# Latent attention in a two-block network: rotary tables built during the feed forward, another order of the projections, one square for four heads, and an exponential issued early

## The chip, the cores and the metric

The kernel runs on one core of one Trainium2 chip. The metric is the device time of one execution in microseconds (us). Differences below about 0.2% (2.5 us of this kernel) can't be told from no change.

## The reference

The network runs 256 tokens of width 1024 through two blocks of two layers each. The first block has a mixer of dilated attention and a state-space scan, then one of gated linear recurrences, each followed by a SwiGLU feed forward of hidden width 2816. The second block has a layer of latent attention and one of grouped-query attention, each with attention over 256 memory tokens beside it, and a feed forward behind each. The change touches mainly the latent attention:

```python
def _mla_mixer(p, q_a_norm, w_q_b, kv_a_norm, w_kv_b, q_norm, k_norm, rope):
    c_q, c_kv, k_pe = p[..., :384], p[..., 384:640], p[..., 640:704]
    q = (_rmsnorm(c_q, q_a_norm) @ w_q_b).reshape(B, S, 8, 128 + 64)
    kv = (_rmsnorm(c_kv, kv_a_norm) @ w_kv_b).reshape(B, S, 8, 128 + 128)
    q_nope = _rmsnorm(q[..., :128], q_norm[:128])
    q_pe = _apply_axial_rope(_rmsnorm(q[..., 128:], q_norm[128:]), rope)
    k_nope = _rmsnorm(kv[..., :128], k_norm[:128])
    v = kv[..., 128:]
    k_pe = _apply_axial_rope(_rmsnorm(k_pe, k_norm[128:])[:, :, None, :], rope)[:, :, 0, :]
    return _blocked_attention([q_nope, q_pe], [k_nope, k_pe], v, 192 ** -0.5)
```

Each head's 128 columns of queries and keys are normalised by their own mean square, and 64 more columns are rotated by tables of cosines and sines (times the norm's gain). The memory queries and the grouped queries are normalised by head too, which needs sums of squares of four heads of 128 columns at a time.

## The kernel before, in words

Tokens lie on the 128 partitions in two halves (`HALVES`). Every product is computed in three matmuls of reduced-precision pieces (`mm3`, L299): the operand and the weights are each split into a high and a low part. A weight tile of 128x1024 holds two blocks of 512 columns; it comes by a DMA of the SP queue into `wr`, ScalarE (ACT) copies it into the high part `wh`, and VectorE (DVE) subtracts to get the low part `wl` (`weights`, L283). Six such pairs and four raw tiles are in flight.

`linear` (L393) issues the weights, then the matmuls of the first half of the tokens, then of the second; behind each half a `sink` takes the PSUM bank (`pm`; there are six) through ACT, DVE and GpSimd (POOL). The sinks of the latent layer, all inside `mla_layer` (L1454):

- `nope_sink` (L1500), for four heads of 128 queries or keys: `normed_heads` (L685) sums the squares of each head (`head_sumsq`, L668), POOL raises them to the power -1/2 (`rsqrt`, L412), DVE multiplies the bank by the factors into a slot `s`, and then TensorE (PE) transposes it into `pt` (against `ident`) and ACT copies it out.
- `rope_sink` (L1513), for the rotated part of all eight heads: the same with eight heads of 64, then `axial` (L770), seven DVE instructions with the tables `rt`, then the transposes.
- `q_mem_sink` (L737) copies the bank, and forms factors of four heads.

`head_sumsq` has two ways: for more than four heads one ACT square over all columns into a scratch tile `j` (there is one such tile) and a DVE reduction (L677); for four or fewer one ACT square for each head, with an accumulated output that a second small ACT instruction reads.

The order of the work is written out by hand. `pe_time` counts the matmuls' modelled time; `later(delay, fn, writes)` queues a step, `poll` (after each `mm3`) issues those that are due, and `need(keys)` forces the steps that write a key. The delays are in `TUNE`: `noden` and `nodego` for the scaling and the transposes of `nope_sink`, `ropen` and `ropego` for the rotary part. The first attention job of the latent layer (`start`, L613) needs the rotated key and queries and the first four heads of plain queries and keys. It is spread right behind the linear that makes the second four heads of keys. The framework's planner then orders each engine's instructions by its own costs, so that one that is written later may stand earlier in its engine's queue.

The order of the linears in the latent layer is: latent queries (3 blocks of 128), latent keys and values with the rotated key, memory queries (L1493), first keys (L1538), rotated queries (L1539), first queries, first values, second keys; then the jobs begin. `rope_tables` (L1438), called at the head of each attention layer, loads gains, cosines and sines, and forms eight products on DVE. The feed forward is `ffn` (L504): its up half runs in chunks of 256 columns with a Silu each, its down half in `rows_out`; an `aside` is called behind its first 512 columns.

Of the kernel before, what the change touches and what calls it, by code (L numbers as in the profile page):

```python
# [9 lines left out]
F32 = mybir.dt.float32  # L10
F32R = mybir.dt.float32r
I32 = mybir.dt.int32
AF = mybir.ActivationFunctionType
# [4 lines left out]
P = 128  # L18
D = 1024
KD = D // P  # L20
FF = 2816
EPS = 1e-6
HALVES = (0, 1)
# [35 lines left out]
    "mqgo": 1.0,  # L59
    "mkn": 3.0,  # L60
    "noden": 2.3,
    "nodego": 3.5,
    "ropen": 2.5,
    "ropego": 5.0,
    "kpego": 3.5,
    "gkn": 2.0,
    "gkgo": 4.0,
# [7 lines left out]
    "conv": 2.3,  # L75
    "mem": 8.0,
    "rows": 2.0,
    "s5a": 0.0,
    "s5ad": 2.0,
    "s5b": 4.5,  # L80
# [61 lines left out]
class Net:  # L142
# [358 lines left out]
            tiles.append(t)  # L501
        return tiles

    def ffn(self, X, r, gate, up, g_at, u_at, down, post, gains, last=False, aside=None):  # L504
        nc = self.nc
        HT = Operand(self, FF // P)
        wg = self.weights([(gate, k * P, g_at, g_at + 512) for k in range(KD)])
        wu = self.weights([(up, k * P, u_at, u_at + 512) for k in range(KD)])
        for h in HALVES:
            G, U = self.group(X, h, wg, 512), self.group(X, h, wu, 512)  # L510
            s, t = self.slot(), self.slot()
            self.act(s, G, AF.Silu, scale=r[h])
            self.mul(t, U, s)
            self.to_features(HT, h, 0, [t[:, i * P : (i + 1) * P] for i in range(4)])
        rows, key = self.spread_rows(r)
        if aside is not None:
            aside()
        mean = [self.sm() for h in HALVES]
        for h in HALVES:
            self.ts(mean[h], r[h], math.sqrt(1.0 / D), ALU.mult)  # L520
        two = lambda a: a.rearrange("p (a q) -> p a q", a=2)
        both = rows.unsqueeze(1).to_broadcast([P, 2, 256])
        for c0 in range(512, FF, 256):
            G = self.wide_t(X, gate, g_at + c0)
            self.need(key)
            s, t = self.slot(), self.slot()
            self.wide_sum(s, G)
            self.mul(two(s), two(s), both)
            self.act(s, s, AF.Silu)
            U = self.wide_t(X, up, u_at + c0)  # L530
            self.wide_sum(t, U)
            self.mul(t, t, s)
            self.heads_out(HT, c0 // P, t)
        gp = None if post is None else self.load_post(post)
        KF = FF // P
        self.flush()
        return self.rows_out(HT, down, range(KF), 5, gp, gains, last, r, mean)
# [130 lines left out]
    def head_sumsq(self, src, nh, dh, r=None):  # L668
        w = self.sm(nh)
        scale = math.sqrt(1.0 / dh)  # L670
        if r is not None:
            scale = self.sm()
            self.ts(scale, r, math.sqrt(1.0 / dh), ALU.mult)
        sq = self.junkt()
        if nh > 4:
            self.act(sq[:, : nh * dh], src, AF.Square, scale=scale)
            self.nc.vector.tensor_reduce(  # L677
                out=w, in_=sq[:, : nh * dh].rearrange("p (n d) -> p n d", n=nh), axis=AX.X, op=ALU.add
            )
        for i in range(nh if nh <= 4 else 0):  # L680
            self.act(sq[:, i * dh : (i + 1) * dh], src[:, i * dh : (i + 1) * dh], AF.Square, scale=scale, accum_out=w[:, i : i + 1])
        self.ts(w, w, EPS, ALU.add)
        return w
# [754 lines left out]
    def rope_tables(self, src, dim, nq):  # L1438
# [4 lines left out]
            self.nc.sync.dma_start(out=pk[i], in_=self.ins[src][i])  # L1443
        at = lambda j: pk[j * dim // 512][:, (j * dim) % 512 : (j * dim) % 512 + dim]
        tabs = {}
        for i, who in enumerate(("q", "k")):
            for h in HALVES:
                C, S = (self.rtab.tile([P, dim], F32, name=self.name("rt"), tag=f"rt{who}{h}{j}") for j in range(2))
                self.mul(C, at(2 * h), at(4 + 2 * i))
                self.mul(S, at(2 * h + 1), at(5 + 2 * i))  # L1450
                tabs[who, h] = (C, S)
        return tabs

    def mla_layer(self, X, R):  # L1454
        tabs = self.rope_tables("rope64", 64, 8)
        CQ, CKV = Operand(self, 3), Operand(self, 2)
        rq, rkv = [None, None], [None, None]

# [31 lines left out]
        self.linear(X, "mla_w_in", 0, 384, latent(CQ, rq, 3, "q_a"))  # L1490
        self.linear(X, "mla_w_in", 384, 704, kv_sink)
        mem = {}
        self.linear(X, "mla_w_in", 704, 1216, self.q_mem_sink(0, R, mem))  # L1493

        qT, kT, V = self.big(), self.big(), self.big()
        qpT = [self.slot(), self.slot()]
# [38 lines left out]
        heads = [job(n) for n in range(8)]  # L1535
        jobs = self.attention(heads[:4] + self.memory_jobs(0, mem, self.mem_kv[0], 8) + heads[4:], Y)
        self.share = TUNE["mla_share"]
        self.linear(CKV, "w_kv_b", 0, 512, nope_sink(kT, rkv, "k_nope", 0, "k"))  # L1538
        self.linear(CQ, "w_q_b", 1024, 1536, rope_sink)  # L1539
        self.linear(CQ, "w_q_b", 0, 512, nope_sink(qT, rq, "q_nope", 0, "q"))  # L1540
        self.linear(CKV, "w_kv_b", 1024, 1536, v_sink(0))
        self.linear(CKV, "w_kv_b", 512, 1024, nope_sink(kT, rkv, "k_nope", 4, "k"))
# [9 lines left out]


    def gqa_layer(self, X, R):
        tabs = self.rope_tables("rope128", 128, 8)
        Y = Operand(self, 12)
        qT, kT, V = self.big(), self.slot(), self.slot()
        head = lambda T, n: T.rearrange("p (n t) -> p n t", n=n)
# [29 lines left out]
        mem = {}  # L1588
# [21 lines left out]
    def run(self):  # L1610
# [19 lines left out]
        self.dump("x_b", X, R)  # L1630
        X, R = self.odd_mixer(X, R)
        self.dump("x_c", X, R)
        X, R = self.ffn(X, R, "gate1", "up1", 0, 0, "down1", 3, "mix2_0")
        self.dump("x_d", X, R)

        X, R = self.mla_layer(X, R)
        self.dump("x_e", X, R)
        X, R = self.ffn(X, R, "gu2_0", "gu2_0", 0, FF, "down2_0", None, "mix2_1")
        self.dump("x_f", X, R)
        X, R = self.gqa_layer(X, R)  # L1640
        self.dump("x_g", X, R)
# [196 lines left out]
```

## Time and profile before

| what | value |
|---|---|
| time, median of 3 runs | 1258.91 us (1258.33 to 1259.23) |
| the profiled execution's own time | 1257.49 us |
| its span from the first to the last instruction | 1255.7 us |
| PE busy, share of the span | 1238.2 us, 99% |
| DVE busy | 879.7 us, 70% |
| ACT busy | 766.5 us, 61% |
| granted clock of PE, mean | 0.999 |
| matmuls | 6526 |

The durations of matmuls overlap, so a busy PE says only that one was under way; what PE loses is read from the distance of one matmul's start to the next one's. An idle time in brackets names the engine and line that ended it. L217 is the helper of every activation, L195 of every two-operand DVE instruction, L208 and L209 of DVE's tensor_scalar, L220 of every matmul, L227 of every transpose, L414 is `rsqrt`: the tile names tell which is which.

### The profile page before, as it was taken

What the parts mean: (1) busy time and instruction counts of PE and PEld (TensorE: products, weight loads), DVE (VectorE), ACT (ScalarE), POOL (GpSimd) and SP (SyncE); (2) the same over time, 40 slices, a digit from 0 to 9 for tenths busy, and PEclk for the clock granted to TensorE, in tenths of its full rate; (3) what the DMA queues carried; (4) which work ended last, traced back from release to release, by engine and by line L of the source; (5) the groups of instructions that cost most, each with busy time, mean ns of one, the idle gap of its engine ahead of it and who ended that gap; (6) DMA issues with size and microseconds to landing.
All of it is one profiled execution on the core that took longest, in us unless ns stands there. A gap on an engine that the chain in (4) does not pass through costs nothing.

```text
span 1255.7 us, 17972 instructions
## 1 busy us (share of the span) xinstructions
PE 1238.2 (99%) x6526; PEld 1036.8 (83%) x6526; DVE 879.7 (70%) x1579; ACT 766.5 (61%) x1446; POOL 52.3 (4%) x64
## 2 busy tenths in 40 slices
PE   8999999999999999999999999999999999999998
PEld 6776888888889788888887788888888888888887
DVE  7897578775588977776477855777746865677752
ACT  6767577554488766555378845555536675655541
POOL 1000000000000100000013100000000100000000
PEclk9999999999999999999999999999999999999999
DMA  8614357666555556666545224656664532666562
GB/s 272 228 54 149 119 200 235 192 193 207 160 184 173 166 187 219 190 193 203 183 151 177 85 68 151 211 191 188 210 191 152 182 118 81 201 199 191 186 196 71
DMA packets 63065, 216.83 MB, mean 173 GB/s; under 512 B 7136, under 2 KB 7520, under 8 KB 62976
## 3 DMA queue, kind: packets, MB, share of 16 engines
q1 hardware_dynamic: 62976, 215.68, 54.2%
q8 instruction: 51, 0.84, 0.3%
q14 instruction: 38, 0.31, 0.1%
HBM read 214.61 MB, written 1.05 MB: 172 GB/s over the span
## 4 chain that ended last, share of the span: by engine, by line
PE 86%; DVE 5%; ACT 4%; DMA 3%; issue 1%; POOL 1%; SPq 0%; ACTq 0%; DVEq 0%; POOLq 0%
PE pm L220 82%; PE pt L227 3%; DVE wl L195 2%; ACT b L217 1%; ACT j L217 1%; DVE s L195 1%; ACT wh L217 1%; ACT s L217 1%; DMA wr<-in_wall_dram 1%; DVE b L212 1%; POOL m L414 1%; DMA s<-in_memT_dram 0%; DMA x<-in_x_dram 0%; DMA s<-in_xT_dram 0%; DMA s<-in_rope_dram 0%
## 5 line engine op out<-in xcount | busy, mean ns | idle before, releaser
L195 DVE TENSOR_TENSOR wl<-wr,wh 128x1024 fp32r<-128x1024 f32 (+2 forms) x389 | 467.2, 1206 | 208.9 <-ACT wh L217 208.1
L220 PE MATMUL pm<-wh,b 128*128 128x512 f32 (+2 forms) x1788 | 574.1, 395 | 3.7 <-ACT wh L217 2.1
L217 ACT ACTIVATE wh<-wr 128x1024 fp32r<-128x1024 f32 (+2 forms) x381 | 397.4, 1047 | 263.7 <-PE pm L220 139.4
L220 PE MATMUL pm<-b,wh 128*128 128x512 f32 (+1 forms) x1440 | 453.2, 372 | 0.0
L220 PEld LDWEIGHTS pm<-wh,b 128*128 128x128 f32 x1788 | 333.7, 188 | 72.6 <-ACT wh L217 4.5
L220 PE MATMUL pm<-b,wl 128*128 128x256 f32 x1296 | 359.6, 278 | 0.0
L220 PE MATMUL pm<-wl,b 128*128 128x512 f32 (+2 forms) x894 | 348.2, 390 | 2.5 <-DVE wl L195 2.5
L220 PEld LDWEIGHTS pm<-b,wh 128*128 128x128 f32 x1440 | 261.1, 188 | 50.7 <-ACT b L217 0.3
L220 PEld LDWEIGHTS pm<-b,wl 128*128 128x128 f32 x1296 | 243.8, 188 | 0.3
L220 PEld LDWEIGHTS pm<-wl,b 128*128 128x128 f32 x894 | 168.2, 188 | 36.6 <-DVE wl L195 5.0
L195 DVE TENSOR_TENSOR s<-pm,s 128x256 f32<-128x256 f32 (+1 forms) x164 | 74.0, 453 | 35.5 <-ACT s L217 19.8
L217 ACT ACTIVATE s<-pm 128x256 f32<-128x256 f32 (+1 forms) x152 | 58.6, 387 | 65.0 <-PE pm L220 64.8
L414 POOL TENSOR_TENSOR m<-m,mhalf 128x1 f32<-128x1 f32 (+3 forms) x54 | 48.2, 892 | 979.6 <-DVE m L209 767.4
L195 DVE TENSOR_TENSOR s<-s,s 128x512 f32<-128x512 f32 (+3 forms) x90 | 60.5, 672 | 2.5
L217 ACT ACTIVATE b<-pt,cpk 128x128 fp32r<-128x128 f32 (+2 forms) x138 | 48.3, 391 | 9.2 <-DVE b L212 5.4
L217 ACT ACTIVATE j<-pm,m 128x128 f32<-128x128 f32 (+1 forms) x94 | 36.8, 406 | 22.3 <-PE pm L220 19.6
L227 PE MATMUL pt<-ident,s 128*128 128x128 f32 x288 | 44.8, 280 | 3.2 <-DVE s L195 1.7
L212 DVE SCALAR_TENSOR_TENSOR b<-pt,cpk,b 128x128 fp32r<-128x128 f32 x122 | 37.9, 344 | 11.7 <-ACT b L217 11.2
L227 PEld LDWEIGHTS pt<-ident,s 128*128 128x128 f32 x288 | 34.7, 144 | 13.7 <-issue 3.1
L217 ACT ACTIVATE j<-x 128x512 f32<-128x512 f32 x32 | 20.2, 631 | 27.2 <-DVE x L212 14.1
L220 PE MATMUL pm<-s,b 128*128 128x256 f32 (+1 forms) x160 | 34.6, 337 | 0.0
L220 PE MATMUL pm<-wr,s 128*128 128x512 f32 x72 | 34.1, 610 | 0.2 <-DMA wr<-in_wall_dram 0.2
(162 smaller groups left out, 810.7 us busy)
## 6 DMA issues: line engine op xcount, KB each, us to landing
wr<-in_wall_dram SPq DMA_DIRECT2D x381, 512.0 KB, 4.1
wr<-in_wall_dram SPq DMA_DIRECT2D x11, 256.0 KB, 3.4
s<-in_memT_dram SPq DMA_DIRECT2D x8, 256.0 KB, 6.1
s<-in_gpost_dram SPq DMA_DIRECT2D x8, 256.0 KB, 5.4
wr<-in_wall_dram SPq DMA_DIRECT2D x4, 384.0 KB, 2.9
x<-in_x_dram SPq DMA_DIRECT2D x2, 512.0 KB, 6.6
s<-in_mem_dram SPq DMA_DIRECT2D x4, 256.0 KB, 5.8
out_dram<-x SPq DMA_DIRECT2D x4, 256.0 KB, 2.0
```

The lines of the kernel that those rows point to most:

```text
L195: return self.nc.vector.tensor_tensor(out=out, in0=a, in1=b, op=op)
L212: return self.nc.vector.scalar_tensor_tensor(out=out, in0=a, scalar=s, in1=b, op0=op0, op1=op1)
L217: return self.nc.scalar.activation(out, a, func, **kw)
L220: self.nc.tensor.matmul(out, lhsT, rhs, start=start, stop=stop)
L227: self.nc.tensor.transpose(out, a, self.ident)
L414: self.nc.gpsimd.tensor_tensor(out=z, in0=w, in1=self.mhalf[:, 0:n], op=ALU.pow)
```

## The change

The rotary tables of both attention layers are loaded in the feed forward ahead of them, and formed 20 us of modelled PE time later. In the latent layer the rotated queries are projected first, then the memory queries, then the first keys. `head_sumsq` takes the way with one square and a reduction from four heads on, at every place that uses it. The feed forward ahead of the latent layer ends its up half with one exponential of a single column, which nothing reads. Three delays are set anew.

```diff
-    "nodego": 3.5,
+    "nodego": 5.0,
-    "ropego": 5.0,
+    "ropego": 8.0,
+    "tabs": 20.0,
...
-    def ffn(self, X, r, gate, up, g_at, u_at, down, post, gains, last=False, aside=None):
+    def ffn(self, X, r, gate, up, g_at, u_at, down, post, gains, last=False, aside=None, then=None):
...
             self.heads_out(HT, c0 // P, t)
+        if then is not None:
+
+            self.act(self.sm(), t[:, 0:1], then, scale=0.0)
         gp = None if post is None else self.load_post(post)
...
-        if nh > 4:
+        if nh >= 4:
             self.act(sq[:, : nh * dh], src, AF.Square, scale=scale)
             self.nc.vector.tensor_reduce(
                 out=w, in_=sq[:, : nh * dh].rearrange("p (n d) -> p n d", n=nh), axis=AX.X, op=ALU.add
             )
-        for i in range(nh if nh <= 4 else 0):
+        for i in range(nh if nh < 4 else 0):
...
         tabs = {}
-        for i, who in enumerate(("q", "k")):
-            for h in HALVES:
-                C, S = (self.rtab.tile([P, dim], F32, name=self.name("rt"), tag=f"rt{who}{h}{j}") for j in range(2))
-                self.mul(C, at(2 * h), at(4 + 2 * i))
-                self.mul(S, at(2 * h + 1), at(5 + 2 * i))
-                tabs[who, h] = (C, S)
+
+        def go():
+            for i, who in enumerate(("q", "k")):
+                for h in HALVES:
+                    C, S = (self.rtab.tile([P, dim], F32, name=self.name("rt"), tag=f"rt{who}{h}{j}") for j in range(2))
+                    self.mul(C, at(2 * h), at(4 + 2 * i))
+                    self.mul(S, at(2 * h + 1), at(5 + 2 * i))
+                    tabs[who, h] = (C, S)
+
+        self.later(TUNE["tabs"], go)
         return tabs
 
+    def remember_tables(self, *args):
+        self.tabs = self.rope_tables(*args)
+
     def mla_layer(self, X, R):
-        tabs = self.rope_tables("rope64", 64, 8)
+        tabs = self.tabs
...
         mem = {}
-        self.linear(X, "mla_w_in", 704, 1216, self.q_mem_sink(0, R, mem))
...
         self.share = TUNE["mla_share"]
+        self.linear(CQ, "w_q_b", 1024, 1536, rope_sink)
+        self.linear(X, "mla_w_in", 704, 1216, self.q_mem_sink(0, R, mem))
         self.linear(CKV, "w_kv_b", 0, 512, nope_sink(kT, rkv, "k_nope", 0, "k"))
-        self.linear(CQ, "w_q_b", 1024, 1536, rope_sink)
         self.linear(CQ, "w_q_b", 0, 512, nope_sink(qT, rq, "q_nope", 0, "q"))
...
     def gqa_layer(self, X, R):
-        tabs = self.rope_tables("rope128", 128, 8)
+        tabs = self.tabs
...
-        X, R = self.ffn(X, R, "gate1", "up1", 0, 0, "down1", 3, "mix2_0")
+        X, R = self.ffn(X, R, "gate1", "up1", 0, 0, "down1", 3, "mix2_0", aside=lambda: self.remember_tables("rope64", 64, 8), then=AF.Exp)
...
-        X, R = self.ffn(X, R, "gu2_0", "gu2_0", 0, FF, "down2_0", None, "mix2_1")
+        X, R = self.ffn(X, R, "gu2_0", "gu2_0", 0, FF, "down2_0", None, "mix2_1", aside=lambda: self.remember_tables("rope128", 128, 8))
```

## Rows read from the trace of the kernel before

**Rows 1.** The page's engines: busy us, share of the span, instructions.
```profile
PE 1238.2 (99%) x6526; PEld 1036.8 (83%) x6526; DVE 879.7 (70%) x1579; ACT 766.5 (61%) x1446; POOL 52.3 (4%) x64
```

**Rows 2.** Stretches: length, busy us of PE, PEld, DVE, ACT, POOL; clock, DMA.
```profile
660.00:680.00 20.00, 19.59 (x91) 15.61 (x91) 12.99 (x36) 17.95 (x58) 5.04 (x5) 1.00 0.53 170
680.00:697.00 17.00, 14.59 (x71) 11.37 (x70) 15.95 (x42) 11.84 (x29) 8.35 (x5) 0.96 0.49 157
404.00:426.00 22.00, 20.56 (x107) 17.22 (x106) 20.86 (x34) 21.59 (x48) 3.54 (x2) 1.00 0.47 149
86.00:98.00 12.00, 11.85 (x78) 7.33 (x77) 11.80 (x25) 7.59 (x25) 1.88 (x2) 1.00 0.30 89
960.00:1000.00 40.00, 40.00 (x190) 33.08 (x189) 33.49 (x86) 27.27 (x72) 5.98 (x7) 1.00 0.57 184
```

**Rows 3.** Timeline of PE in the latent layer: start, us, what, idle before it.
```profile
649.97 0.91 PE L220 MATMUL pm<-wh,b 128*128 128x384 f32 x4 [0.21 <-DVE b L212]
...
692.51 0.39 PE L220 MATMUL pm<-wl,b 128*128 128x512 f32 x1
692.74 0.39 PE L220 MATMUL pm<-wh,b 128*128 128x512 f32 x1
694.24 0.63 PE L227 MATMUL pt<-ident,s 128*128 128x128 f32 x4 [1.11 <-DVE m L208]
695.97 1.94 PE L227 MATMUL pt<-ident,s 128*128 128x128 f32 x8 [1.10 <-DVE s L195]
697.83 1.22 PE L220 MATMUL pm<-b,b 128*128 128x256 f32 x2
...
705.04 1.13 PE L220 MATMUL pm<-b,s 128*128 128x256 f32 x4 [0.85 <-DVE s L195]
```

**Rows 4.** Timeline of DVE there and at the tables of the grouped layer.
```profile
648.48 1.18 DVE L195 TENSOR_TENSOR rt<-s 128x64 f32<-128x64 f32 x8 [0.62 <-DMA s<-in_rope_dram]
...
682.03 0.68 DVE L677 TENSOR_REDUCE m<-j 128x8 f32<-128x512 f32 x1
682.63 0.68 DVE L195 TENSOR_TENSOR wl<-wr,wh 128x512 fp32r<-128x512 f32 x1
...
693.42 0.67 DVE L195 TENSOR_TENSOR s<-s,s 128x512 f32<-128x512 f32 x1
...
695.13 1.28 DVE L195 TENSOR_TENSOR s<-pm,m 128x512 f32<-128x512 f32 x2
...
903.08 1.29 DVE L195 TENSOR_TENSOR rt<-s,s 128x128 f32<-128x128 f32 x6
```

**Rows 5.** What DVE waited for from 660 to 697: us, times, longest.
```profile
DVE m L208 <- ACT j L217: 3.2, 4, 1.3
DVE m L209 <- POOL m L414: 2.4, 2, 1.2
```

**Rows 6.** Timeline of ACT: one sink's squares, a square of eight heads, the exponential's table, the feed forward's end.
```profile
676.06 0.37 ACT L217 ACTIVATE j<-pm,m 128x128 f32<-128x128 f32 x1 [0.24 <-DVE m L208]
...
677.45 1.06 ACT L217 ACTIVATE wh<-wr 128x1024 fp32r<-128x1024 f32 x1
...
680.71 0.72 ACT L217 ACTIVATE j<-pm,m 128x512 f32<-128x512 f32 x1
681.28 0.67 ACT L217 ACTIVATE wh<-wr 128x512 fp32r<-128x512 f32 x1
...
702.88 1.28 ACT L217 ACT_TABLE_LOAD   x1
704.17 0.47 ACT L217 ACTIVATE s<-pm,m 128x256 f32<-128x256 f32 x1
...
587.27 1.06 ACT L217 ACTIVATE wh<-wr 128x1024 fp32r<-128x1024 f32 x1 [1.66 <-PE pm L220]
```

**Rows 7.** Timeline in the recurrent mixer, DVE and then PE.
```profile
424.63 1.20 DVE L195 TENSOR_TENSOR wl<-wr,wh 128x1024 fp32r<-128x1024 f32 x1
...
425.88 0.50 PE L220 MATMUL pm<-wl,b 128*128 128x512 f32 x1 [1.44 <-DVE wl L195]
```

## The prediction

> **What bounds the kernel now.** The first view is the page's table of engines: PE is under way for 1238.2 of 1255.7 us, so only what makes PE wait, or run slower, can change the time [rows 1]. The second is the table of stretches. The reader is to see that PE has no wait in most of them (40.00 of 40.00 from 960 to 1000), and loses most between 680 and 697, where it is busy for 14.59 of 17 us and the clock is below full. In those 17 us DVE is busy for 15.95, and just ahead, from 660 to 680, for 12.99 of 20 [rows 2]. The third is PE's timeline around 693: matmuls of 512 columns start 0.23 us apart (692.51, 692.74); then comes a wait to 694.24 and, behind four transposes, one to 695.97, and the first scores start at 697.83 [rows 3]. The two idle times add up to 2.21 us; counted by starts (1.50 less 0.23, and 1.73 less four transposes of some 0.1) the loss is about 2.6. The transposes that wait belong to the rotated queries and the first plain queries, which the first attention job forces; both waits end on DVE. The fourth view, DVE's timeline and its waits, says why: the last addition of the rotary part runs at 693.42 and the scaling of the plain queries at 695.13 [rows 4], so DVE is behind there, after having stood idle earlier, for squares of ACT (3.2 us) and for factors of POOL (2.4) [rows 5]. So the stretch is set by how DVE's work is spread, not by PE.
>
> The terms below are of the profiled execution: a span of 1255.7 us, 1257.49 as its own time. The median of the runs shown is 1258.91, 1.42 above it; I take the difference that I forecast off that median.
>
> **Tables early.** In the latent layer eight products of 1.18 us together run at 648.48, after 0.62 of waiting for their DMA, and behind them stand DVE's parts of the operand, for which PE waits 0.21 at 649.97 (counted by starts, 0.4) [rows 3, 4]. Moved into the feed forward, this wait goes: -0.3, between -0.4 and 0. The table for grouped attention already runs at 903.08, in the feed forward [rows 4]: 0. The three loads of 256 KB pass SP's queue ahead of weight tiles there; ACT stands idle 1.66 us per weight tile for PE to free one [rows 6], so the weights are ahead of PE and a late tile is covered: 0, and at most the 0.6 of that same DMA wait if the cover is gone.
>
> **Exponential early.** Its table load of 1.28 us at 702.88 lies right ahead of the first softmax at 704.17 [rows 6], and PE waits 0.85 at 705.04 for a scaling on DVE that came late in the same tangle [rows 3]. At the end of the up half ACT's 1.66 us of idle for each weight tile takes a load of 1.28. Between it and the softmax come squares and copies, none of which loads a table in the trace between 640 and 702. I take 0.6 of the 0.85 as returned, together with the shorter squares on ACT: -0.6, between -0.85 and 0 (the wait names DVE, not ACT).
>
> The row puts nothing behind the load: 702.88 and 1.28 give 704.16, and the exponential starts at 704.17 [rows 6]. The Trainium skill (ScalarE: Activation LUTs, What ACT_TABLE_LOAD costs) wants some 1.38 us of drain beside the load, 2.66 for a switch; by it up to 1.4 more would be taken from ACT's chain, at most the whole 0.85 of PE. The trace doesn't show the drain, so the sum stands on the row.
>
> **One square for four heads.** Today a sink takes ACT from 676.06 to 677.45, 1.39 us. The one square of 512 columns for eight heads holds it from 680.71 to 681.28, 0.57. DVE pays a reduction, 682.03 to 682.63, 0.60 [rows 6, 4]. There are 20 such sinks: 4 of memory keys, 4 of memory queries, 8 in the latent layer, 4 of grouped queries; ACT loses 16 us and DVE gains 12. What it is worth depends on who is behind. In the grouped layer DVE is busy 33.49 of 40 us and PE never waits [rows 2]; four reductions by 1000 (2.4 us) and the two of its memory queries later fit: 0, up to +0.5. In the recurrent mixer DVE is busy 20.86 of 22 us [rows 2], and PE waits 1.44 at 425.88 for a low part that DVE does at 424.63, last in its queue [rows 7]. Two reductions come ahead of it. If both push it, +1.2; if the planner puts the low part ahead, 0. I take half, +0.6. In the first layer DVE is busy 11.80 of 12 us beside the memory keys [rows 2], with two reductions more; most of what PE does there doesn't wait on them: +0.3, between 0 and +0.7.
>
> The one scratch tile adds a wait: a square of ACT must now let the previous reduction of DVE finish. Behind a square that waits stand the high parts `wh`, hence the low parts, hence PE. Today's squares already wait for a small DVE instruction of their own sink, so I price it within the next term.
>
> **Rotated queries first.** For each half the rotary part takes DVE a reduction, a scaling, a full product and an addition of 512 columns (0.6 to 0.67 each), four products of a quarter (an estimate of 0.2 each) and small ones (0.3): some 3.5 us, 7 us in all. They move from the stretch where DVE is full to the one where it has 7 us idle (20 less 12.99) [rows 2, 4]. What the first job then waits for is the plain queries alone. Where does DVE reach their scaling? Today at 695.13 to 696.3. Up to there DVE has done 28.9 us of work in 37 and was idle 8.1 [rows 2]. The work grows by six reductions (memory queries, first keys, first queries), 3.6. The idle time shrinks: four waits for squares, 3.2 us, lose 0.8 each, some 2.5, and waits for POOL, of which 2.4 us are in one group [rows 5], are filled with rotary work, if that is in the queue: between 0 and 2.4, and I take half, 1.2. So DVE ends at 696.3 + 3.6 - 2.5 - 1.2 = 696.2 less the 0.3 of the tables, 695.9, and the first of the two scalings 0.64 earlier, 695.2. PE, freed of the first 0.3 and with the rotary transposes done earlier (the same work), is there at about 693. The rest of the reductions' chain is nearly unchanged: a square and a reduction (1.2) for four squares (1.39).
>
> That would leave a wait of 2.2, almost all of today's. But two things make it shorter. DVE's own waits before 680 came with an empty queue; with seven us of rotary work in it, the waits for ACT there vanish wholly rather than by 0.8. And POOL's factor, for which the scaling waits, follows a square that comes 0.8 earlier. I take 1.2 as the wait that stays, of 2.6: -1.4. Bounds: all of it goes, -2.6; or no idle time is filled and DVE ends 3.6 later, +3.6.
>
> **The clock.** It is 0.96 over 17 and over 23 us [rows 2]: 0.04 of 40 us, 1.6 us of full speed lost to a fall to the lower level (1.2 GHz), behind the two waits. In the recurrent mixer a single wait of 1.44 passes at clock 1.00 [rows 2, 7]. With one wait of about 1.2 left I expect no fall: -1.6, or 0 where the wait stays at two us or more.
>
> Sum: -0.3 - 0.6 + 0.6 + 0.3 - 1.4 - 1.6 = -3.0, that is 1254.5 for a profiled execution and **1255.9** for the median. Its own range, with half of the clock's 1.6 and half of the recurrent mixer's 1.2 either way, is 1254 to 1258.
>
> **Rivals.**
> - *All of it returns* (14%). Both waits at 693, the clock, the wait at 705 and the tables go, and nothing is pushed elsewhere: -0.4 - 2.6 - 1.6 - 0.85 = -5.4, 1253.5. For it: DVE's 7 us of idle from 660 to 680. Against: six reductions go into the same queue.
> - *The wait changes its owner* (26%). The plain queries come as late as the rotated ones did, by the count of 2.2 above; the clock falls again. What is left is -0.3 - 0.6 from tables and exponential against +0.9 from the reductions elsewhere: 0, 1258.9. This is also the case in which the planner orders the queues as before, so that the change doesn't do what it says.
> - *DVE becomes the bound* (13%, slower). The place is DVE's queue from 660 to 697: if its 8.1 us of idle time don't shrink, since the high parts that it waits for stand on ACT behind squares that wait for reductions, it ends 3.6 late. Then PE waits 6.2 where it lost 2.6, the clock falls as today, and the recurrent and first mixers cost their full 1.2 and 0.7: +3.6 + 1.9 - 0.9 = +4.6, 1263.5. It decides from the point at which DVE's idle time shrinks by less than the 3.6 us of reductions. Against it: 3.2 us of that idle time are waits for the very squares that get shorter.
> - The forecast has 47%.
>
> **How the numbers follow.** About 0.2% (2.5 us) can be told from no change. Faster than 1256.4: all of the first rival, and some 40 of the forecast's 47 in 100, less what the planner may cost elsewhere: 0.53. Slower than 1261.4: 0.13. Within: 0.34. The range leaves out the slower rival and the far end of the first, with 1.5 below 1253.5 for what another order of the queues may win where no term is priced: 1252.0 to 1261.0.
>
> **What would show it.** Right: in the changed trace the rotary reductions and products lie between 663 and 677; the transposes ahead of the first scores wait once, for a scaling, by about 1.2; the clock stays full from 640 to 720; no table load stands ahead of the first softmax, and one of 1.28 lies near 583 with no PE wait behind it; PE's wait near 425 has grown by 0.6. Wrong: two waits there, or a clock below full; DVE idle for more than 5 us between 660 and the first scores; PE waiting for `wl` between 660 and 690, which is the slower rival; a PE wait in the feed forward behind the load or the tables.

## The result, and the profile after

The changed kernel takes 1273.41 us (median of 4 runs, 1270.42 to 1275.47), the kernel before beside it 1258.62 (4 runs). The ratio is 1.0125 (95% interval 1.0110 to 1.0139): slower by 1.25%. The forecast was 1255.9, the range ended at 1261.0. The profiled execution took 1272.6 us, with a span of 1270.8.

The page's engines, after (columns as in [rows 1]):

```profile
PE 1241.2 (98%) x6526; PEld 1037.5 (82%) x6526; DVE 893.0 (70%) x1599; ACT 751.2 (59%) x1307; POOL 53.8 (4%) x64
```

The work did change as the prediction counted it. ACT has 139 instructions and 15.3 us less, DVE 13.3 us more, PE the same 6526 matmuls. The reductions are one group of DVE, 20 new ones and the two of eight heads that were there before (out<-in, times, then busy us, mean ns, idle ahead and its cause):

```profile
L681 DVE TENSOR_REDUCE m<-j 128x4 f32<-128x512 f32 (+1 forms) x22 | 15.0, 680 | 7.6 <-ACT j L218 7.5
```

The stretches of the latent layer, after (columns as in [rows 2]):

```profile
660.00:680.00 20.00, 19.37 (x94) 15.56 (x93) 15.98 (x50) 14.84 (x34) 6.39 (x6) 1.00 0.48 160
680.00:690.00 10.00, 9.16 (x47) 7.33 (x46) 8.28 (x17) 5.04 (x9) 2.56 (x2) 1.00 0.53 152
690.00:700.00 10.00, 6.58 (x30) 4.91 (x29) 8.23 (x16) 6.53 (x9) 4.21 (x3) 1.00 0.66 231
700.00:710.00 10.00, 6.47 (x23) 4.89 (x23) 5.60 (x17) 3.90 (x6) 3.02 (x3) 0.68 0.21 65
```

From 660 to 680 DVE is busy for 3 us more than before; the rotary work was counted at 7. But between 690 and 710 PE is busy for 13.05 of 20 us, and in the last ten of them DVE is busy for 5.60 and ACT for 3.90: the three wait for one another. The clock falls to 0.68 from 700 to 710, part of it at the lower level (1.2 GHz): 3.2 us of full speed, where it was 1.6. That is 0.04 of the 17 us to 697 [rows 2] and of the 23 us behind them, whose row in the kernel before is this:

```profile
697.00:720.00 23.00, 22.15 (x114) 18.54 (x113) 17.63 (x56) 21.64 (x73) 4.03 (x4) 0.96 0.29 92
```

PE's timeline there, and after it PE in the recurrent mixer; these answer to [rows 3] and to PE's row of [rows 7]:

```profile
694.50 0.50 PE L221 MATMUL pm<-wh,b 128*128 128x512 f32 x1 [2.73 <-ACT b L218]
...
698.22 0.63 PE L228 MATMUL pt<-ident,s 128*128 128x128 f32 x4 [0.69 <-DVE s L196]
...
701.68 0.63 PE L228 MATMUL pt<-ident,s 128*128 128x128 f32 x4 [0.78 <-DVE s L196]
...
705.06 1.94 PE L228 MATMUL pt<-ident,s 128*128 128x128 f32 x8 [2.75 <-DVE s L196]
...
719.06 1.07 PE L228 MATMUL pt<-ident,s 128*128 128x128 f32 x8 [1.20 <-DVE s L209]
720.91 0.66 PE L228 MATMUL pt<-ident,s 128*128 128x128 f32 x4 [0.78 <-ACT b L218]
722.49 1.13 PE L221 MATMUL pm<-s,b 128*128 128x256 f32 x4 [0.92 <-ACT s L218]
...
428.58 0.50 PE L221 MATMUL pm<-wl,b 128*128 128x512 f32 x1 [1.21 <-DVE wl L196]
```

What PE waits for is seen on ACT and DVE, first ACT, then DVE (answers to [rows 6] and [rows 4]):

```profile
690.72 0.69 ACT L218 ACTIVATE j<-pm,m 128x512 f32<-128x512 f32 x1 [3.25 <-DVE m L209]
691.30 1.99 ACT L218 ACTIVATE wh<-wr 128x1024 fp32r<-128x1024 f32 x2
693.20 0.68 ACT L218 ACTIVATE j<-pm,m 128x512 f32<-128x512 f32 x1
693.76 1.26 ACT L218 ACTIVATE b<-pm,m 128x512 f32<-128x512 f32 x2
```

```profile
690.34 0.23 DVE L210 TENSOR_SCALAR m<-m,m 128x4 f32<-128x4 f32 x1 [1.12 <-POOL m L415]
690.48 0.15 DVE L209 TENSOR_SCALAR m<-m 128x1 f32<-128x1 f32 x1
691.44 0.69 DVE L681 TENSOR_REDUCE m<-j 128x4 f32<-128x512 f32 x1 [0.81 <-ACT j L218]
...
692.38 2.36 DVE L196 TENSOR_TENSOR wl<-wr,wh 128x1024 fp32r<-128x1024 f32 x2
...
704.09 0.23 DVE L209 TENSOR_SCALAR m<-m,m 128x4 f32<-128x4 f32 x1 [1.39 <-POOL m L415]
704.23 1.28 DVE L196 TENSOR_TENSOR s<-pm,m 128x512 f32<-128x512 f32 x2
```

Read backwards from 694.50: PE waits 2.73 us for ACT's copies `b` of the values, which free its banks. They stand in ACT's queue behind the square at 690.72, and that one stood for 3.25 us until DVE had done a scale of one column (690.48). The scale stood in DVE's queue behind a factor that waited 1.12 for POOL, whose input is the sum of an earlier square. One tile's square, reduction, factor and the next tile's square thus follow each other through three queues, and what stands behind them in each queue waits too.

Where the time went, by places. All traces have the same number of matmuls, so the start of the n-th is compared with its start in the kernel before. The cells are us lost (+) or won, between the matmuls that lie at these times in the kernel before, from one profiled execution each. Where the order of the projections differs, the n-th matmul isn't the same work, so there only the sum from 669 to 734 counts. The first 31 us differ by -1.1 to +3.2 from one execution to the next, whatever the kernel, and say nothing.

| place | changed | squares alone | idle reductions | new order, squares apart | the same, old delays | changed, old delays |
|---|---|---|---|---|---|---|
| 94 to 131, first mixer | +1.8 | +1.8 | +0.8 | 0 | 0 | +1.8 |
| 669 to 691 | +4.1 | +0.7 | +0.4 | +1.9 | +3.2 | +9.1 |
| 691 to 706 | +1.4 | +2.7 | +3.4 | -3.0 | -3.6 | -4.6 |
| 706 to 734 | +3.4 | +1.2 | 0 | +3.2 | +0.3 | +0.4 |
| 969 to 1032, grouped | +2.0 | +2.0 | +0.7 | 0 | 0 | +2.0 |

### The profile page after: what moved, and what is told of

Its sections match the earlier page's. It is cut to its first block, busy times and chain, and to the rows that moved or that the text cites. A ratio compares the mean times of both kernels' runs of the same rounds, so it can differ in the third digit from the quotient of the medians.

```text
span 1270.8 us, 17872 instructions
## 1 busy us (share of the span) xinstructions
PE 1241.2 (98%) x6526; PEld 1037.5 (82%) x6526; DVE 893.0 (70%) x1599; ACT 751.2 (59%) x1307; POOL 53.8 (4%) x64
## 4 chain that ended last, share of the span: by engine, by line
PE 76%; DVE 6%; ACT 4%; issue 2%; POOL 1%; DMA 1%; ACTq 0%; DVEq 0%; POOLq 0%
PE pm L221 73%; PE pt L228 3%; DVE wl L196 2%; DVE s L196 2%; ACT wh L218 1%; POOL m L415 1%; ACT b L218 1%; ACT j L218 1%; ACT s L218 1%; DMA wr<-in_wall_dram 1%; DVE m L681 1%; DVE b L213 0%; ACT L218 0%; DVE b L1430 0%; DVE m L209 0%
## 5 line engine op out<-in xcount | busy, mean ns | idle before, releaser
L218 ACT ACTIVATE j<-pm,m 128x512 f32<-128x512 f32 (+1 forms) x34 | 22.1, 652 | 29.5 <-PE pm L221 18.7
L218 ACT ACTIVATE s<-pm,m 128x256 f32<-128x256 f32 (+3 forms) x42 | 23.4, 566 | 18.8 <-DVE m L209 12.3
```

What stands on the lines that cost most here:

```text
L218: return self.nc.scalar.activation(out, a, func, **kw)
```

## The experiments

Eighteen kernels ran. Ratios are against the kernel before on the same chip, with 95% intervals.

**The parts of the change.** The theory: the merged squares cost, since a square that needs DVE before and after it puts ACT and DVE in series. The rival: the new order does.

`e1_no_merged_squares`, the changed kernel with

```
-        if nh >= 4:
+        if nh > 4:
...
-        for i in range(nh if nh < 4 else 0):
+        for i in range(nh if nh <= 4 else 0):
```

> The changed kernel with the four squares of a sink apart again; new order, early tables and early exponential stay. Theory S (the merged square costs the time: DVE gets a reduction of 0.6 us for each sink, and the next sink's square on ACT stands behind DVE's queue, as where ACT waits 3.25 us ahead of 690.72 in the changed trace): the 14.8 us go, 1254 to 1259. Theory O (the new order costs it: all plain queries and keys are now projected in one burst just ahead of the first job): about 1268 to 1273.

Measured 1260.16 us, 1.0028 (1.0017 to 1.0038).

`e2_squares_alone`, the kernel before with the squares merged and nothing else:

```
-        if nh > 4:
+        if nh >= 4:
...
-        for i in range(nh if nh <= 4 else 0):
+        for i in range(nh if nh < 4 else 0):
```

> The kernel before with the merged squares alone; old order, old delays, tables at the layer's head. Theory S: most of the loss, 1267 to 1273. Theory O: 1257 to 1261, since the order is the old one.

Measured 1267.10 us, 1.0079 (1.0060 to 1.0098).

`e3_old_order`, the changed kernel with the latent layer's order and its two delays as before:

```
-    "nodego": 5.0,
+    "nodego": 3.5,
...
-    "ropego": 8.0,
+    "ropego": 5.0,
...
+        self.linear(X, "mla_w_in", 704, 1216, self.q_mem_sink(0, R, mem))
...
-        self.linear(X, "mla_w_in", 704, 1216, self.q_mem_sink(0, R, mem))
         self.linear(CKV, "w_kv_b", 0, 512, nope_sink(kT, rkv, "k_nope", 0, "k"))
+        self.linear(CQ, "w_q_b", 1024, 1536, rope_sink)
```

> The changed kernel with the old order of the linears and the old two delays; merged squares, early tables and early exponential stay. Theory S: 1266 to 1272, little better than the changed kernel. Theory O: 1255 to 1259.

Measured 1268.10 us, 1.0081 (1.0063 to 1.0098).

`e4_tables_and_exp_alone`, the change without its squares, order and delays, that is only the early tables and the early exponential:

> Early tables and early exponential alone: old order, old delays, squares apart. Both theories: 1257 to 1259, 0 to 1 us below the kernel before (the 0.3 and 0.6 of the prediction); more than 1261 would mean that these two parts cost time, which no theory of mine has.

Measured 1258.01 us, 1.0005 (0.9996 to 1.0014).

So the tables and the exponential give nothing that can be told from zero, the squares cost 0.8% with either set of the other edits in the old order, and the order with its delays costs 0.2 to 0.4% more. The squares are the larger part, the order with its delays a smaller one; whether a series of two engines is what makes the squares dear is the next question.

**Why the squares cost.** Three causes can be told apart: the one scratch tile `j` (M1), the scale of one column (M2), DVE's reductions (M3).

`f1_two_scratch_tiles`, on `e2_squares_alone` (the pool of small tiles cut from 48 to 44 to make room):

```
-        self.junk = e(tc.tile_pool(name="junk", bufs=1))
+        self.junk = e(tc.tile_pool(name="junk", bufs=2))
```

> The kernel before with the squares of four heads in one activation (1267.1 us when alone), and a second scratch tile j, so that a square no longer waits until VectorE has reduced the one ahead of it. Theory M1 (the one scratch tile makes ScalarE's next square wait): 1257 to 1261 us. Theory M2 (the 128x1 scale that each square needs stands in VectorE's queue behind wide work): 1264 to 1268, since a square still waits for its scale. Theory M3 (the reductions that VectorE has to do and wait for are the cost): 1265 to 1268.

Measured 1267.76 us, 1.0082 (1.0062 to 1.0102).

`f2_scale_once`, on `e2_squares_alone`:

```
-            scale = self.sm()
-            self.ts(scale, r, math.sqrt(1.0 / dh), ALU.mult)
+            if (id(r), dh) not in self.scales:
+                scale = self.sm()
+                self.ts(scale, r, math.sqrt(1.0 / dh), ALU.mult)
+                self.scales[id(r), dh] = (r, scale)
+            scale = self.scales[id(r), dh][1]
```

> The kernel before with the merged squares and one scratch tile, but the 128x1 scale of a row of factors worked out once and kept, where each sink of it worked it out again. M2: 1257 to 1261 us. M1: 1264 to 1268, since the square then waits for the reduction ahead of it instead. M3: 1265 to 1268.

Measured 1265.33 us, 1.0057 (1.0040 to 1.0073).

`f3_two_tiles_scale_once`, both:

> Both of the last two: two scratch tiles and the scale kept. M1 or M2, alone or as a pair that needs both: 1256 to 1260 us, ScalarE's waits for VectorE ahead of j (0.88 to 3.45 us) gone from the stretch from 669 to 734. M3: 1264 to 1268 with those waits gone and PE's waits for VectorE still there.

Measured 1266.61 us, 1.0075 (1.0050 to 1.0100).

`f4_idle_reductions`, the kernel before, with

```
+        if nh == 4:
+            self.nc.vector.tensor_reduce(out=self.sm(4), in_=self.ident.unsqueeze(1).to_broadcast([P, 4, P]), axis=AX.X, op=ALU.add)
```

> The kernel before, squares apart as they were, and beside each four of them one more reduction of 128x4 from 128x512 on VectorE whose result nobody reads and which waits for nothing: VectorE's added work alone (22 x about 0.6 us = 13 us). M3 in its plain form (VectorE's time): 1264 to 1268 us. M1, M2, or a reduction that costs because it has to wait for a square: 1258 to 1261.

Measured 1265.52 us, 1.0054 (1.0036 to 1.0073).

M1 falls. M2 falls as the main cause; whether the scale is worth the 0.2% between 1.0079 and 1.0057 isn't settled, the intervals overlap and the pair of edits gave 1.0075. M3 stands: 20 reductions (13.5 us of DVE in all) that wait for nothing and that nobody reads cost two thirds of what the merged squares do. In that trace PE waits like this (timeline of PE):

```profile
698.55 0.63 PE L227 MATMUL pt<-ident,s 128*128 128x128 f32 x4 [1.56 <-DVE m L208]
702.14 1.09 PE L227 MATMUL pt<-ident,s 128*128 128x128 f32 x4 [2.97 <-DVE m L208]
```

The squares alone have the same two waits, with no idle reduction in them:

```profile
696.28 0.63 PE L227 MATMUL pt<-ident,s 128*128 128x128 f32 x4 [1.57 <-DVE m L208]
...
700.11 1.09 PE L227 MATMUL pt<-ident,s 128*128 128x128 f32 x4 [3.20 <-DVE m L208]
```

But DVE's timeline with the idle reductions shows more than added time:

```profile
686.36 0.68 DVE L677 TENSOR_REDUCE m<-j 128x8 f32<-128x512 f32 x1
686.95 0.68 DVE L195 TENSOR_TENSOR wl<-wr,wh 128x512 fp32r<-128x512 f32 x1
...
689.03 1.23 DVE L195 TENSOR_TENSOR wl<-wr,wh 128x1024 fp32r<-128x1024 f32 x1 [0.45 <-ACT wh L217]
...
690.77 1.21 DVE L195 TENSOR_TENSOR wl<-wr,wh 128x1024 fp32r<-128x1024 f32 x1
...
692.78 1.22 DVE L195 TENSOR_TENSOR wl<-wr,wh 128x1024 fp32r<-128x1024 f32 x1
...
694.51 0.68 DVE L683 TENSOR_REDUCE m<-ident 128x4 f32<-128x512 f32 x1
...
696.58 1.22 DVE L195 TENSOR_TENSOR wl<-wr,wh 128x1024 fp32r<-128x1024 f32 x1
...
699.19 0.68 DVE L683 TENSOR_REDUCE m<-ident 128x4 f32<-128x512 f32 x1
...
701.30 0.69 DVE L195 TENSOR_TENSOR s<-s,s 128x512 f32<-128x512 f32 x1
```

From the first reduction of eight heads to the end of the last rotary sum DVE takes 15.55 us (686.36 to 701.91), where it took 11.99 before (682.03 to 694.02, [rows 4]), and it has next to no idle time in either. Of these 3.56 us the two idle reductions are 1.18, and 2.27 are two more low parts of 128x1024 (four, where there were two). In the kernel before those two stand behind the scaling of the plain queries; with the reductions the planner wrote them ahead of the rotary sums. The squares alone have the same: 15.68 us, four low parts, two reductions. So in this stretch a third of the growth is the added work and two thirds is the other order of DVE's queue. That is read from the queues; no kernel ran with the reductions and the old order of the low parts.

**Taking work off DVE.** If DVE's queue is the limit there, less of it should give time back. Four kernels tried.

`g4_low_parts_on_gpsimd`, on `e4_tables_and_exp_alone` (and `g1_squares_low_parts_on_gpsimd` on `f2_scale_once`, with the first plain queries' weights as well):

```
-            self.sub(lo[:, :n], raw[:, :n], hi[:, :n].bitcast(F32))
+            (self.low or self.nc.vector).tensor_tensor(out=lo[:, :n], in0=raw[:, :n], in1=hi[:, :n].bitcast(F32), op=ALU.subtract)
...
+        self.low = self.nc.gpsimd
         self.linear(CQ, "w_q_b", 1024, 1536, rope_sink)
+        self.low = None
```

> The kernel before with early tables and the exponential (ratio 1.0005), and the low parts of the rotary queries' weights (1.23 and 0.68 us on VectorE) on GpSimd. If VectorE's time from 684 to 705 already sets PE's waits near 693 and 695 (2.6 us together) and near 704: 1255.5 to 1257.5 us, ratio 0.998 to 0.999. If it has slack there until the squares' reductions come: 1257 to 1260, ratio 0.9995 to 1.001. If GpSimd is too late: over 1260, PE waiting for wl.

> The kernel before with the merged squares and the scale worked out once (1265.3 us), and with the low parts (raw minus high, the 128x1024 and 128x512 subtractions into wl) of the weights of the rotary queries and of the first content queries on GpSimd instead of VectorE: some 3.7 us of VectorE's work (two pairs of 1.23 and 0.68) leave the stretch from 684 to 705 in which it has no idle time. If VectorE's time there is the cost: back by about as much as the squares put in there, to 1259 to 1263 us, VectorE idle again between 690 and 705. If the cost is a chain of waits between ScalarE and VectorE: 1264 to 1268. Rival: GpSimd takes so long for a low part that PE waits for wl instead: over 1266, with PE waiting for wl of POOL.

Measured 1260.49 us, 1.0025 (1.0016 to 1.0035), and 1269.47 us, 1.0096 (1.0081 to 1.0112). Both took the work from the wrong place: these weights are prepared from 661 on, not at 690. Both kernels lose 3.3 to 3.6 us between 658 and 669. Why is in the first one's timelines of POOL, DVE and PE:

```profile
661.26 3.19 POOL L296 TENSOR_TENSOR wl<-wr,wh 128x1024 fp32r<-128x1024 f32 x1 [0.45 <-ACT wh L219]
...
662.15 2.73 DVE L197 TENSOR_TENSOR s<-s,rt 128x64 f32<-128x64 f32 x5
...
667.04 0.57 DVE L197 TENSOR_TENSOR s<-s,rt 128x64 f32<-128x64 f32 x5
...
665.56 0.78 PE L229 MATMUL pt<-ident,s 128*128 128x128 f32 x3 [2.33 <-DVE m L210]
```

Five products with the tables (one of 128x64 and four of 128x16, merged in these rows) take DVE 2.73 us while POOL subtracts, and 0.57 when it doesn't; PE then waits 2.33. The rival named for these runs (PE waits for `wl` of POOL) isn't what happened. The two runs leave the question of DVE's queue at 690 open.

`h1_scaling_on_scalar`, on `e4_tables_and_exp_alone`, for the latent layer's plain queries and keys:

```
+                for n in range(nh):
+                    self.act(out[:, n * dh : (n + 1) * dh], src[:, n * dh : (n + 1) * dh], scale=f[:, n : n + 1])
```

> The kernel before with early tables and the exponential (ratio 1.0005), and the scaling of the latent layer's eight tiles of four content heads on ScalarE (four activations of 128x128) instead of VectorE (one product of 0.69 us): 0.69 x 8 = 5.5 us off VectorE, some 1.2 x 8 = 10 us onto ScalarE. If VectorE's queue already sets PE's waits between 690 and 705 before the change: 1253 to 1257, ratio 0.996 to 0.999, VectorE idle there. If VectorE only becomes the bound through the added reductions: ratio 0.999 to 1.002. If ScalarE has no room for it: above 1.003.

Measured 1265.29 us, 1.0067 (1.0050 to 1.0084).

`h2_squares_and_scaling_on_scalar`, the same edit on `e2_squares_alone`:

> The kernel before with the merged squares (1267.1 us, ratio 1.0079), and the same eight scalings on ScalarE: the 0.69 us that each takes off VectorE stand against the 0.60 that a reduction adds. If VectorE's time in the latent layer is the cost of the merged squares there (some 5 of their 8 to 10 us): 1260 to 1263, ratio 1.002 to 1.004, the rest being the first and the grouped layer. If the cost is that each square needs both engines in turn: 1265 to 1268.

Measured 1270.65 us, 1.0116 (1.0101 to 1.0132).

Neither theory of the second run expected that the scaling would cost on top of the squares (1.0116 against 1.0079); of the first, the third of its cases came true, though not for want of room on ACT. ACT's timeline of the first, and what it does to PE:

```profile
696.90 1.14 ACT L218 ACTIVATE s<-pm,m 128x128 f32<-128x128 f32 x4 [4.19 <-DVE m L209]
...
696.87 1.09 PE L228 MATMUL pt<-ident,s 128*128 128x128 f32 x4 [4.14 <-DVE m L209]
```

ACT had room, 4.19 us of it, but spent it at the head of its queue, waiting for the factor that DVE's full queue gave late. A further hand-over between the two cost more than the work that it moved.

`i1_no_cast_on_vector`, on the kernel before, and `i2_squares_no_cast_on_vector`, on `e2_squares_alone`:

```
-    "mla_share2": 0.25,
+    "mla_share2": 0.0,
```

> The kernel before, squares apart, with nothing else changed than that VectorE makes none of the high parts of the out projection's weights: the cast of 0.68 us at 692.82 (and those at 718.82 and 750.54) becomes an activation of 1.05 us, which waits for nothing but its weights' transfer. VectorE's queue from 680 to 698.7 gets 0.68 us shorter without a new wait behind it. If that queue sets PE's waits near 695 and 697: 1255.5 to 1257.5 us, ratio 0.998 to 0.9995, PE's waits near 694.6 and 703.8 shorter by some 0.6 each. If it does not: ratio 0.9995 to 1.001 with those waits unchanged. If ScalarE has no room (it has 4.1 us idle between 689 and 697): above 1.001.

> The kernel before with the merged squares (ratio 1.0079) and the same three casts on ScalarE. If VectorE's time in the stretch from 680 to 705 is the cost of the merged squares there: 1263 to 1266 us, ratio 1.005 to 1.007 (0.7 to 2 us less). If it is the chain between the two engines: 1266 to 1268.5, ratio 1.007 to 1.009.

Measured 1258.75 us, 1.0009 (1.0000 to 1.0018), and 1266.16 us, 1.0074 (1.0061 to 1.0087). Nothing came back. DVE's queues, as built, show why (the kernel before with -, the first of the two with +):

```
 TENSOR_SCALAR m<-m 128x4
-CAST wh<-wr 128x1024
+TENSOR_TENSOR wl<-wr,wh 128x1024
 TENSOR_TENSOR s<-s,s 128x512
```

The low part of the same weights, ready sooner, took the cast's place, 1.21 us for 0.68, ahead of the sum that PE waits for. DVE's and PE's timelines of that kernel (against 693.42 and the wait of 1.11 in [rows 4, 3]):

```profile
692.66 1.21 DVE L195 TENSOR_TENSOR wl<-wr,wh 128x1024 fp32r<-128x1024 f32 x1
693.79 0.68 DVE L195 TENSOR_TENSOR s<-s,s 128x512 f32<-128x512 f32 x1
...
694.62 0.63 PE L227 MATMUL pt<-ident,s 128*128 128x128 f32 x4 [1.63 <-DVE m L208]
```

**Why the order costs.** `g2_new_order_old_delays`, on `e1_no_merged_squares` (and `h4_changed_old_delays`, on the changed kernel):

```
-    "nodego": 5.0,
+    "nodego": 3.5,
...
-    "ropego": 8.0,
+    "ropego": 5.0,
```

> The changed kernel with the squares apart again (1260.2 us, ratio 1.0028) and the two delays back at 3.5 and 5.0: early tables, exponential and the new order alone. If the longer delays are what the order costs: ratio 1.000 to 1.0015. If the order itself: 1.002 to 1.004. If the longer delays save something: above 1.004.

Measured 1258.26 us, 1.0009 (0.9999 to 1.0020).

`g3_rotary_ahead_of_keys`, `e4_tables_and_exp_alone` with one step of the order:

```
-        self.linear(CKV, "w_kv_b", 0, 512, nope_sink(kT, rkv, "k_nope", 0, "k"))
         self.linear(CQ, "w_q_b", 1024, 1536, rope_sink)
+        self.linear(CKV, "w_kv_b", 0, 512, nope_sink(kT, rkv, "k_nope", 0, "k"))
```

> The kernel before with early tables and the exponential (ratio 1.0005), and of the new order one step alone: the rotary queries ahead of the content keys, the memory queries where they were, old delays. If this step is what the order costs: ratio 1.002 to 1.004 with VectorE late around 680. If the memory queries' move is: 0.999 to 1.001.

Measured 1261.69 us, 1.0040 (1.0025 to 1.0055).

> The changed kernel (1273.4 us, ratio 1.0125) with the two delays back at 3.5 and 5.0. If the longer delays cost the same with the merged squares as without (1.0028 against 1.0009, some 2.4 us): 1270 to 1272, ratio 1.010 to 1.011. If the delays are what the new order and the squares cost together (1.0125 - 1.0081 = 0.0044, some 5.5 us): 1267 to 1269. If they cost nothing beside the squares: 1272 to 1275.

Measured 1266.37 us, 1.0081 (1.0066 to 1.0096).

The order alone costs nothing that can be told from zero (1.0009 beside the 1.0005 of tables and exponential), and of its two steps the move of the memory queries makes up for the other. The longer delays do cost: 1.0028 against 1.0009 without the squares (their intervals just overlap, and the places from 706 to 734 agree), 1.0125 against 1.0081 with them. In the kernel with squares apart and long delays, PE's waits behind 706 are these:

```profile
708.69 1.06 PE L228 MATMUL pt<-ident,s 128*128 128x128 f32 x8 [0.94 <-DVE s L209]
710.54 0.66 PE L228 MATMUL pt<-ident,s 128*128 128x128 f32 x4 [0.78 <-ACT b L218]
712.11 1.13 PE L221 MATMUL pm<-s,b 128*128 128x256 f32 x4 [0.92 <-ACT s L218]
```

With the old delays that kernel has no wait from 702 to 736; it loses 0.3 from 706 to 734 where this one loses 3.2. In the changed kernel the same three waits stand at 719.06, 720.91 and 722.49. The changed kernel with old delays has its largest wait, 5.84 us for a tile that DVE scales, at 695.75: the delays don't make the squares' cost, they add to it.

`h3_new_order_idle_reductions`, on `e1_no_merged_squares`, with the idle reductions of `f4_idle_reductions`:

> The changed kernel with the squares apart (ratio 1.0028) and one idle reduction on VectorE beside each four of them: as the changed kernel for VectorE's work, without the chain from square to reduction. If VectorE's time is what the squares cost in the new order too: 1268 to 1273, ratio 1.008 to 1.0125. If the chain is: 1260 to 1264.

Measured 1266.26 us, 1.0083 (1.0067 to 1.0100): the idle reductions cost 0.0055 here (over 1.0028) and 0.0054 on the kernel before. The rest, from 1.0083 to 1.0125, is what the squares cost beyond DVE's work when the delays are long. The chain read above in the changed kernel's queues may be it; no run isolates it.

No version beat the kernel before. Tables and exponential alone (1.0005), and with the new order at the old delays (1.0009), are the same as it.

## Why the prediction was wrong

The table sums it up. The shares are differences of the ratios above, of 1258 us; by the intervals each is uncertain by some 2 us.

| part | forecast, us | measured | from |
|---|---|---|---|
| tables and exponential | -0.9 | +0.6 | `e4_tables_and_exp_alone` |
| order, old delays | -1.4 and -1.6 of clock, with the squares | +0.5 | `g2_new_order_old_delays` less that |
| longer delays | none | +2.4 | `e1_no_merged_squares` less that |
| squares | +0.9 elsewhere, the rest within -1.4 | +9.1 | `h4_changed_old_delays` less `g2_new_order_old_delays` |
| delays and squares together | none | +3.1 | what is left of 1.0125 |

- **The step that failed** is the count under "Rotated queries first" that brings DVE to the plain queries' scaling at 695.9: "The work grows by six reductions", "The idle time shrinks", so -1.4, and with it "One square for four heads", which passed its wait on to that count. DVE gets there at 704.23. At 660 PE's matmuls start 3.0 us later in the changed trace, so 657 to 695.13 before is the same piece of work of PE as 660 to 704.23 after (175 matmuls in both; columns as in [rows 2]; before, then after):

```profile
657.00:695.13 38.13, 36.14 (x175) 28.82 (x173) 28.95 (x84) 32.42 (x96) 14.85 (x13) 1.00 0.55 173
660.00:704.23 44.23, 36.63 (x175) 28.62 (x174) 35.12 (x91) 27.78 (x52) 15.17 (x12) 0.99 0.53 174
```

  DVE's work ahead of the scaling grew by 6.2 us, where 3.6 were counted, and its idle time went from 9.18 to 9.11, where it was to shrink by 3.7. So DVE comes 6.1 us later than it did, by PE's time, and by the places the stretch from 669 to 734 lost 8.9 us in place of the -1.4 and -1.6. The rotary work did fill the stretch from 665 to 682, but with 2.41 us of waits of its own in it; up to the scaling DVE's waits for ACT fell from 4.2 to 3.4 us, and those for POOL's factors rose from 4.6 to 5.9.
- What the count left out is the order of DVE's queue. It added durations as though the work ahead of the scaling stayed the same. With the reductions, two low parts of 1.13 moved ahead of it, and in the two kernels of the old order read above they took more of DVE than the two reductions beside them (2.27 against 1.18). In the changed kernel it is the same number: DVE has done 220 low parts when it reaches the scaling, where it had done 218. Six reductions (3.8) and two low parts (2.3) make up 6.0 of the 6.2.
- It took the wait for a small DVE instruction ahead of each square as a price of today that stays. The rows after show 3.25 us for one such instruction.
- **"One scratch tile adds a wait"** was a wrong lead: a second tile gave 1.0082 against 1.0079 (on the squares alone).
- **The clock's** -1.6 didn't come, since the waits didn't shrink: the loss grew from 1.6 to 3.2.
- **The other layers** were priced +0.6 (recurrent), +0.3 (first) and 0 (grouped). The recurrent wait is 1.21 where it was 1.44 [rows 7], so that term is 0. The first mixer loses 1.8, although DVE was known to be full there [rows 2]. Of it 0.8 comes near 95, and the idle reductions cost as much. The second square of the memory keys stands 3.47 us for DVE's scale, behind products of 0.66, but that isn't the other 1.0: by 112 ACT is level with PE again (its copy `b<-pm` at 112.09, where it was at 110.28, and PE is 1.8 later too). The 1.0 comes near 128, where PE waits 1.34 for ACT, which falls behind from 114 on: its second copies from `pt` start at 118.38, where they started at 113.89, since ACT and PE have another order there. No run isolates that. The grouped layer loses 2.0, with 1.04 of it in one wait of PE where there was none; its 33.49 of 40 us were read as room, but the reductions lie on the way from a projection to its transposes. Rows of ACT and then of PE, after:

```profile
97.25 0.69 ACT L218 ACTIVATE j<-pm,m 128x512 f32<-128x512 f32 x1 [3.47 <-DVE m L209]
...
128.59 0.93 PE L228 MATMUL pt<-ident,s 128*128 128x128 f32 x6 [1.34 <-ACT s L218]
...
1001.75 0.63 PE L228 MATMUL pt<-ident,s 128*128 128x128 f32 x4 [1.04 <-DVE s L196]
```

- **Tables and exponential** moved as said: the load of 1.28 us stands alone at 586.68 and the tables at 487.8, with no wait of PE by them. Where they stand alone (`e4_tables_and_exp_alone`), the wait of 0.85 at 705.04 [rows 3] is gone and 691 to 706 is 0.7 shorter, yet 706 to 734 is 1.4 longer, so the -0.9 didn't arrive. The return of a wait that is not the last one in its tangle was counted as time.

```profile
586.68 1.28 ACT L218 ACT_TABLE_LOAD   x1
```

- **The longer delays** stood in the diff and had no term at all. They cost 2.4 us alone and more beside the squares.
- Of the rivals, *DVE becomes the bound* was on the right side, with its point of decision met: from 660 to 697 DVE's idle time fell from 8.06 us to 6.93, by 1.1, which is less than 3.6. Its price of +4.6 is near the 5.3 us of the idle reductions' column above, but 10 us short of what was measured. Its mechanism, high parts on ACT behind squares, is a small part: DVE's waits for `wh` up to the scaling rose from 0.7 to 1.8 us, and its sign isn't seen, as PE never waits for `wl` between 660 and 705. It had 13%, since waits for squares were expected to shrink with the squares. ACT's squares did shrink; what that gave went into the waits for POOL's factors.

## What to carry to other kernels

An operation moved from an engine with idle time in the average to one that is full just where PE waits was paid twice here: by its duration, and by what the planner then wrote ahead of the late work in that engine's queue. So count what stands in the in-order queue between the last two things that PE waits for, one by one, and take the order after the change as unknown: both ends of a forecast should hold one or two of the largest instructions that may move in. And a hand-over between engines cost not the 0.15 us of its instruction but the queue in front of it and behind it (3.25 us at 690.72); work that is done in one engine, even more than twice as long on it (1.39 us for 0.57 here), can be the cheaper one.

## What was not expected of the hardware

A small product on DVE stands still beside a subtraction of two operands on POOL. In `g4_low_parts_on_gpsimd` the five small products took 2.73 us beside it and 0.57 after it; 2.39 of the 2.73 are the first product alone, which ended 0.09 us after POOL's subtraction did. In `g1_squares_low_parts_on_gpsimd` the same product stands 2.39 (at 668.21) beside a subtraction of 2.38. POOL's subtraction in the first kernel took 3.19 us, and it had begun while DVE was at a low part of its own; with no such work on DVE one of the same size took 2.40 (at 677.16 in the second; POOL's spans are rough). The Trainium skill (SBUF — State Buffer, SBUF: two separate sides) says that VectorE and GpSimd share one pair of ports, which the one that starts first holds for its whole instruction, on VectorE's side when it reads two operands from SBUF, and that the other is blocked meanwhile. The rows agree with that.

The same shows in the changed kernel itself. POOL's factor of four heads takes 1.01 us at most places, but 1.85, 2.00 and 1.90 at 684.51, 692.47 and 696.16, each begun during one of DVE's low parts; the first of them is in the chain read backwards from 694.50. In the kernel before, only one such factor between 660 and 705 is that long (1.92 at 693.04). So a low part that moves ahead can also lengthen the factor that the next scale waits for; what that is worth no run isolates. Two rows of POOL, after:

```profile
684.51 1.85 POOL L415 TENSOR_TENSOR m<-m,mhalf 128x4 f32<-128x4 f32 x1 [8.16 <-ACT s L218]
...
689.29 1.01 POOL L415 TENSOR_TENSOR m<-m,mhalf 128x4 f32<-128x4 f32 x1 [2.93 <-DVE m L209]
```
